# A two-layer trunk on one core: in the channel mixers, every other inner tile as seven block products, the residual kept in DRAM, and rho applied behind the second half

## The chip, the core and the metric

The kernel runs on one core of one Trainium2 chip. Such a core has a matrix engine (TensorE: PE in the profile, with PEld for its weight loads), three elementwise engines (VectorE: DVE; ScalarE: ACT; GpSimd: POOL), a queue that issues transfers (SyncE: SP), and DMA engines between DRAM and the on-chip memory SBUF. TensorE writes its results into PSUM, of which this program uses eight banks of 128 x 512 float32 in the channel mixers, and DVE and ACT read them there. Every engine works through its own instructions in order, and waits at semaphores for the others.

The metric is the device time of one execution in microseconds. Before the change it is 1362.86 us, the median of three runs (1361.54 to 1366.15).

## The reference

Two layers over 512 frames of width 1024. Layer 0 mixes time by a recurrence, layer 1 by chunked attention; the change touches neither. Each layer ends in a channel mixer with an inner width of 2816:

```python
def rms_norm(x, g):
    y = xf * lax.rsqrt(jnp.mean(xf * xf, axis=-1, keepdims=True) + RMS_EPS)
    return y * g

def conv_glu(h, w_in, conv_w, conv_b, w_out):
    gate, val = jnp.split(h @ w_in, 2, axis=-1)
    gp = jnp.pad(gate, ((0, 0), (CONV_W - 1, 0), (0, 0)))
    conv = conv_b + sum(conv_w[j] * gp[:, j:j + seq] for j in range(CONV_W))
    return (jax.nn.gelu(conv, approximate=False) * val) @ w_out

for layer in range(DEPTH):
    ...
    x = x + jnp.concatenate([mix, mo], axis=-1) @ w_out[layer]
    x = x + conv_glu(rms_norm(x, ln2[layer]), ffn_in[layer], ffn_conv[layer],
                     ffn_conv_b[layer], ffn_out[layer])
return rms_norm(x, ln_f)
```

## The kernel before, in words

Everything is stored with features on the 128 partitions and the 512 frames along the free axis: `xT`, the residual, is eight tiles of 128 x 512. A float32 product is made of three products of float32r halves: an operand is split into a rounded part (`whi`, `r1h`) and the rest (`wlo`, `r1l`), and `dense` (L189 to L204) issues, for every block of 128 input features, hi x hi (L198) and hi x lo (L199), and after all of them lo x hi (L203). One unit of eight blocks is thus 16 + 8 matmuls of 128 x 512.

A weight block is loaded by SP into `wraw` (L180, two buffers), cast by ACT to `whi` (L169) and subtracted by DVE to `wlo` (L175). `whi` and `wlo` have three buffers each, so the cast for a unit waits until the matmuls of the third unit before it have read theirs.

`ffn(l, ...)` is the channel mixer. Its input is x times the gain `ln2`, split, without the factor `rho` (the reciprocal root of the mean square, one number per frame), which commutes with the products and is multiplied in afterwards. It has two halves:

- The first half runs over 22 inner tiles j. Each makes two units, the gate into one PSUM bank (`psf`, four banks) and the value into another, then on DVE and ACT: gate times `rho` (L355), the three convolution taps (L357 ACT, L358 and L359 DVE), Gelu (L360 ACT), value times `rho` (L362), their product (L363), and its split into the hidden tile (L215 ACT, L216 DVE). Hidden tiles 0 to 7 lie in the pair of buffers that the other mixer stage uses (`r1h`/`r1l` or `r2h`/`r2l`), 8 to 21 in `f3h`/`f3l`.
- The second half runs over eight output tiles m, each 22 blocks (66 matmuls) into one of two banks `psd`, which DVE adds to `xT[m]` (L374); then the norm's squares and the next stage's input follow (`norm_tile`, L230 to L236).

In layer 1 the last output tile goes through `finish`: two halves of 256 frames, each 66 matmuls of 128 x 256, so that norm and output of the first half lie beside the matmuls of the second.

The Tile framework's scheduler decides the order on each engine from the order of the calls, the pools' buffers and its own estimates; the order is fixed when the program is built.

Of the kernel before, what the change touches and what calls it, by code (L numbers as in the profile page):

```python
# [39 lines left out]
for _n, _c in _VEC:  # L40
# [71 lines left out]
def trunk_kernel(ctx, tc, A, out):  # L112
# [13 lines left out]
    cst = cp.tile([P, NCST], F32, name="cst")  # L126
# [213 lines left out]
    def ffn(l, hp, act, h_, l_, xT, after, last=None):  # L340
        f3h = hp.tile([P, NFF - 8, S], F32R, name="f3h")
        f3l = hp.tile([P, NFF - 8, S], F32R, name="f3l")

# [3 lines left out]
        for j in range(NFF):  # L347
            wg = load_w(A["ffn_in"][l, j, 0])
            wv = load_w(A["ffn_in"][l, j, 1])
            pg = ps_f()  # L350
# [4 lines left out]
            V.tensor_tensor(g[:], pg[:], rho[:], op=ALU.mult)  # L355
# [4 lines left out]
            SC.activation(c[:], c[:], AF.Gelu)  # L360
# [2 lines left out]
            V.tensor_tensor(v[:], v[:], c[:], op=ALU.mult)  # L363
            split_to(*hid(j), v[:])
        for m in range(KD):
# [8 lines left out]
            V.tensor_tensor(xT[:, m], xT[:, m], ps[:], op=ALU.add)  # L374
            after(m)
# [928 lines left out]
```

## Time and profile before

| view | |
|---|---|
| median of 3 runs | 1362.86 us |
| the profiled execution | 1368.61 us, of which the span from first to last instruction 1366.8 |
| DVE | 827.0 us busy, 61% |
| ACT | 609.7 us busy, 45% |
| POOL | 35.2 us busy, 3% |
| DMA | 140.49 MB, mean 103 GB/s |
| 22 inner tiles of layer 0 | from 403.1 to 642.5 us |
| 8 output tiles of layer 0 | to 763 us |
| attention of layer 1 | to about 957 us |
| 22 inner tiles of layer 1 | from 963.7 to 1203 us |
| 8 output tiles of layer 1, norm and output | to the end |

The profile is one execution taken by the hardware profiler, and runs a little longer than the median run. Times in its rows are counted from the first instruction. In a row of the timeline stand start, duration, engine, line of the source, operation, what is written from what, shapes, how many such instructions the row holds, and in brackets how long the engine idled before it and what ended that. Engines start the next instruction before the last one has quite ended, so the distance from start to start is shorter than the duration: for one DVE instruction of 128 x 512 by some 0.08 us.

### The profile page before, as it was taken

How to read it: one execution, taken by the hardware profiler on the slowest of the kernel's cores; microseconds unless marked ns; L12 is line 12 of the kernel's file. 1: busy time of each engine (PE TensorE's matmuls, PEld its weight loads, DVE VectorE, ACT ScalarE, POOL GpSimd, SP SyncE). 2: the span in 40 equal slices, each digit the busy share in tenths (PEclk: the TensorE clock that was granted, in tenths of full speed). 3: DMA queues.
4: the chain of work that ended last, by engine and by line, in shares of the span. 5: the costliest groups of instructions: out<-in, count | busy, mean ns of one | idle time of the engine just before them, and what ended most of it. 6: DMA issues, size and time to landing. Idle time of an engine off the chain costs nothing.

```text
span 1366.8 us, 20878 instructions
## 1 busy us (share of the span) xinstructions
PE 1318.4 (96%) x8266; PEld 1072.8 (78%) x8266; DVE 827.0 (61%) x1751; ACT 609.7 (45%) x1019; POOL 35.2 (3%) x57
## 2 busy tenths in 40 slices
PE   6989999999999999999999999999999999999996
PEld 5777777776788888888888878786888888888886
DVE  7876888788565655655334666757665555653324
ACT  5556554545444333333222476657443333332221
POOL 3000000000000000000000000000000000000000
PEclk9999999999999999999999999999999999999998
DMA  5366544545222232223323422231322232232332
GB/s 182 105 187 138 106 100 96 126 109 131 78 93 93 93 107 94 93 98 97 85 85 111 133 86 87 92 115 63 108 93 93 93 108 93 93 94 87 108 85 75
DMA packets 64322, 140.49 MB, mean 103 GB/s; under 512 B 24672, under 2 KB 28896, under 8 KB 64224
## 3 DMA queue, kind: packets, MB, share of 16 engines
q1 hardware_dynamic: 61200, 128.15, 29.9%
q0 software_dynamic: 3024, 11.01, 4.7%
q8 instruction: 65, 1.06, 0.3%
q14 instruction: 33, 0.27, 0.1%
HBM read 132.32 MB, written 6.82 MB: 102 GB/s over the span
## 4 chain that ended last, share of the span: by engine, by line
PE 78%; DVE 12%; ACT 4%; DMA 3%; issue 2%; SPq 1%; DVEq 0%; ACTq 0%; POOLq 0%
PE psf L198 12%; PE psf L199 12%; PE psf L203 12%; PE psd L198 10%; PE psd L199 10%; PE psd L203 9%; DVE Xu L675 2%; DVE Xs L677 1%; PE pss L1121 1%; PE psl L203 1%; DMA d<-Xs 1%; PE pss L725 1%; DMA Tt<-d 1%; PE pss L297 1%; PE psd L1071 1%
## 5 line engine op out<-in xcount | busy, mean ns | idle before, releaser
L175 DVE TENSOR_TENSOR wlo<-wraw,whi 128x1024 fp32r<-128x1024 f32 (+1 forms) x181 | 216.5, 1196 | 134.0 <-PE psd L203 122.5
L169 ACT CAST whi<-wraw 128x1024 fp32r<-128x1024 f32 (+1 forms) x202 | 207.7, 1029 | 161.1 <-DMA wraw<-in_ffn_out_dram 40.0
L198 PE MATMUL psf<-r1h,whi 128*128 128x512 f32 x352 | 137.2, 390 | 0.0
L198 PE MATMUL psf<-r2h,whi 128*128 128x512 f32 x352 | 137.2, 390 | 0.0
L199 PE MATMUL psf<-r1l,whi 128*128 128x512 f32 x352 | 137.0, 389 | 0.0
L199 PE MATMUL psf<-r2l,whi 128*128 128x512 f32 x352 | 137.0, 389 | 0.0
L198 PE MATMUL psd<-r1h,whi 128*128 128x512 f32 x318 | 127.8, 402 | 1.2 <-ACT whi L169 1.2
L199 PE MATMUL psd<-r1l,whi 128*128 128x512 f32 x318 | 125.4, 394 | 0.0
L203 PE MATMUL psd<-r1h,wlo 128*128 128x512 f32 x318 | 86.7, 405 | 4.4 <-DMA wlo<-in_wA_dram 4.4
L199 PE MATMUL psd<-f3l,whi 128*128 128x512 f32 (+1 forms) x238 | 88.6, 377 | 0.0
L198 PE MATMUL psd<-f3h,whi 128*128 128x512 f32 (+1 forms) x238 | 88.6, 377 | 0.0
L362 DVE TENSOR_TENSOR tmp<-psf,rho 128x512 f32<-128x512 f32 x44 | 30.4, 691 | 94.6 <-PE psf L203 94.6
L203 PE MATMUL psf<-r1h,wlo 128*128 128x512 f32 x352 | 86.9, 389 | 0.0
L203 PE MATMUL psf<-r2h,wlo 128*128 128x512 f32 x352 | 86.9, 389 | 0.0
L198 PE MATMUL psd<-r2h,whi 128*128 128x512 f32 (+1 forms) x200 | 77.1, 389 | 0.8 <-ACT r2h L1128 0.7
L199 PE MATMUL psd<-r2l,whi 128*128 128x512 f32 (+1 forms) x200 | 76.4, 385 | 0.8 <-DVE r2l L216 0.8
L198 PEld LDWEIGHTS psf<-r1h,whi 128*128 128x128 f32 x352 | 66.1, 188 | 13.8
L203 PEld LDWEIGHTS psf<-r1h,wlo 128*128 128x128 f32 x352 | 66.1, 188 | 13.7
L203 PEld LDWEIGHTS psf<-r2h,wlo 128*128 128x128 f32 x352 | 66.1, 188 | 13.7
L198 PEld LDWEIGHTS psf<-r2h,whi 128*128 128x128 f32 x352 | 66.1, 188 | 13.7
L199 PEld LDWEIGHTS psf<-r2l,whi 128*128 128x128 f32 x352 | 66.1, 188 | 13.6
L199 PEld LDWEIGHTS psf<-r1l,whi 128*128 128x128 f32 x352 | 66.1, 188 | 13.6
(368 smaller groups left out, 2440.4 us busy)
## 6 DMA issues: line engine op xcount, KB each, us to landing
wraw<-in_ffn_in_dram SPq DMA_DIRECT2D x88, 512.0 KB, 3.2
wraw<-in_ffn_out_dram SPq DMA_DIRECT2D x32, 448.0 KB, 3.3
wraw<-in_wA_dram SPq DMA_DIRECT2D x20, 512.0 KB, 4.0
wlo<-in_wA_dram POOLq DMA_DIRECT2D x17, 512.0 KB, 8.2
wraw<-in_w_out_dram SPq DMA_DIRECT2D x16, 512.0 KB, 3.5
wraw<-in_ffn_out_dram SPq DMA_DIRECT2D x16, 512.0 KB, 4.3
wraw<-in_wB_dram SPq DMA_DIRECT2D x8, 512.0 KB, 3.4
Lr<-d SPq DMA_DIRECT2D x24, 128.0 KB, 5.4
```

The source lines that it names most:

```text
L169: SC.copy(hi[:, :n], raw)
L175: V.tensor_tensor(lo[:, :n], raw, hi[:, :n], op=ALU.subtract)
L198: PE.matmul(ps, wh[:, j * P:(j + 1) * P], ah, start=start and n == 0, stop=False)
L199: PE.matmul(ps, wh[:, j * P:(j + 1) * P], al, start=False, stop=False)
L203: PE.matmul(ps, wl[:, j * P:(j + 1) * P], act(k)[0], start=False, stop=stop and n == len(ks) - 1)
L297: PE.matmul(pso[hs, :], vm[l][:, kt, (f * 2 + hh) * 64:(f * 2 + hh + 1) * 64], pts[f, hh, kt], start=kt == 0, stop=kt == 1)
L362: V.tensor_tensor(v[:], pv[:], rho[:], op=ALU.mult)
L675: V.tensor_tensor(uv, L1.rearrange("p i o -> p o i").to_broadcast([P, k, n]), X[:, 0:k, q:q + 1].to_broadcast([P, k, n]), op=ALU.mult)
L677: V.tensor_tensor(X[:, 0:k, q + 1:], X[:, 0:k, q + 1:], uv, op=ALU.add)
L725: PE.matmul(ps[h][:, c], KB[HS[h], cc, 1 - h:3 - h].rearrange("p s t -> p (s t)"), AR[HS[h], cc].rearrange("p s t -> p (s t)"), start=True ...
L1071: PE.matmul(pt, r1h[:, k, ts], wh[:, ws], start=k == 0, stop=False)
L1121: PE.matmul(pso[HS[hh], kt * P:], vS[i // 2][:, kt, (i % 2 * 2 + hh) * 64:(i % 2 * 2 + hh + 1) * 64], pts[hh][:, kt, kt * P:], start=kt == ...
```

## The change

**Seven products.** For j = 4, 6, ..., 16 (seven tiles in each layer) the two units of an inner tile are computed as a 2 x 2 block product. The blocks of one factor are the input's upper and lower 512 features for the first and last 256 frames (B00, B10, B01, B11), those of the other the gate and value weights for the upper and lower features. Seven block products, each 4 blocks of 128 features in three passes, 12 matmuls of 128 x 256, replace eight. They need four sums of input blocks (T1 to T4) and sums of weight blocks: `seven` forms them from the raw weights on DVE and splits four sets, `wv`, `wg`, `wx` and `w4`. The products run as: b = B00·wv; c = T1·wg; b += T2·wx; a = B10·wv; b += T3·wx; b += T4·wg; c += B11·w4. After the first, second and third step ACT copies the running sum out of bank b (s0, s1, u0), DVE combines these copies with a and c, and matmuls go on adding into the same bank.

**Order.** `ffn` runs a seven up to T3, then the first 12 matmuls of the next tile's gate unit, then T4 and w4, then the rest of that tile.

**Sums of the input.** `sums`, called behind tiles 0 and 1, reads x back from DRAM, scales by `ln2`, forms T1 to T4 and splits them: the rounded parts into `xh`, which takes the place of `xT` in SBUF, the rests into slots of `f3h`/`f3l` that belong to hidden tiles 18 to 21.

**The residual.** POOL stores `xT` to DRAM (`xd`, 8 transfers) ahead of the mixer and loads it back behind tile 17 (8 transfers). To make room, the constants of which only the first layer has need (`cs2`) are in a tile of that stage.

**rho.** The value is no longer multiplied by `rho`; each of the second half's outputs is, ahead of the residual add (one DVE instruction more for each m, one less for each plain tile).

```diff
+    SEVEN = range(4, 18, 2)
+    HT = (slice(0, 256), slice(256, 512))
-    def ffn(l, hp, act, h_, l_, xT, after, last=None):
+    def ffn(l, hp, ih, il, h_, l_, xT, after, last=None):
...
+        xd = dp.tile([KD, P, S], F32, name="xd", tag="xd", bufs=2)
...
+        def sums(k):
+            u, w = tmp(), tmp()
+            for t_, q in ((u, k), (w, k + 4)):
+                nc.sync.dma_start(t_[:], xd[q])
+                SC.activation(t_[:], t_[:], AF.Copy, scale=Vc(f"ln2_{l}", q))
+            t12, t34 = tmp(), tmp()
+            V.tensor_tensor(t12[:, HT[0]], u[:, HT[1]], u[:, HT[0]], op=ALU.subtract)
...
+            for n, t_ in enumerate((t12, t34)):
+                split_to(high(k)[:, n], low(k)[:, n], t_[:])
...
+        def prod(ps, w, o, a, start=True):
+            wh, wl = w
+            for k in range(4):
+                ws = slice(o + k * P, o + k * P + P)
+                ah, al = a(k)
+                PE.matmul(ps, wh[:, ws], ah, start=start and k == 0, stop=False, skip_group_check=not start)
+                PE.matmul(ps, wh[:, ws], al, start=False, stop=False, skip_group_check=not start)
+            for k in range(4):
+                PE.matmul(ps, wl[:, o + k * P:o + k * P + P], a(k)[0], start=False, stop=k == 3,
+                          skip_group_check=not start)
...
+        def seven(j):
+            rv = hp.tile([P, 1024], F32, name="rv", tag="rv")
+            rg = hp.tile([P, 1024], F32, name="rg", tag="rg")
...
+            wv = split_w(rv[:], 1024)
+            V.tensor_tensor(rg[:, one], rg[:, one], rg[:, two], op=ALU.add)
+            wg = split2(own("wg", 1024), rg[:])
+            V.tensor_tensor(rg[:, one], rg[:, one], rv[:, one], op=ALU.subtract)
+            V.tensor_tensor(rg[:, two], rg[:, two], rg[:, one], op=ALU.subtract)
+            V.tensor_tensor(rv[:, two], rv[:, two], rg[:, one], op=ALU.subtract)
+            wx = split_w(rg[:], 1024)
+            w4 = split2(own("w4", 512), rv[:, two])
...
+            prod(b[:], wv, 0, B(0, 0))
+            SC.copy(s[:, HT[0]], b[:])
+            yield
+            prod(c[:], wg, 0, T(1))
+            prod(b[:], wx, 0, T(2), False)
+            SC.copy(s[:, HT[1]], b[:])
+            a = ps_f((P, 256))
+            prod(a[:], wv, 512, B(1, 0))
+            V.tensor_tensor(v[:, HT[0]], a[:], s[:, HT[0]], op=ALU.add)
+            prod(b[:], wx, 512, T(3), False)
+            u = tmp()
+            SC.copy(u[:, HT[0]], b[:])
+            V.tensor_tensor(u[:, HT[1]], c[:], u[:, HT[0]], op=ALU.add)
+            V.tensor_tensor(g[:, HT[1]], u[:, HT[1]], rho[:, HT[1]], op=ALU.mult)
+            yield
+            prod(b[:], wg, 512, T(4), False)
+            V.tensor_tensor(g[:, HT[0]], b[:], rho[:, HT[0]], op=ALU.mult)
+            prod(c[:], w4, 0, B(1, 1), False)
+            V.tensor_tensor(v[:, HT[1]], c[:], s[:, HT[1]], op=ALU.add)
+            gated(j, g, v[:])
...
+            if j == SEVEN[-1] + 1:
+                xT = mid.tile([P, KD, S], F32, name="xT", tag="xT")
+                for m in range(KD):
+                    GP.dma_start(xT[:, m], xd[m])
...
-            V.tensor_tensor(xT[:, m], xT[:, m], ps[:], op=ALU.add)
-            after(m)
+            t = tmp()
+            V.tensor_tensor(t[:], ps[:], rho[:], op=ALU.mult)
+            V.tensor_tensor(xT[:, m], xT[:, m], t[:], op=ALU.add)
+            after(xT, m)
```

What the scheduler makes of it is seen on the two engines that feed TensorE. On ACT before, one inner tile of layer 0 (hidden tile 13 from `tmp_5998`, tile 14's convolution in `tmp_6067`) has two casts of weights, the cast of the hidden tile, the first tap and Gelu:

```order
L169 CAST whi_6079<-wraw_6077 128x1024
L215 CAST f3h_4965<-tmp_5998 128x512
L169 CAST whi_6085<-wraw_6083 128x1024
L357 ACTIVATE tmp_6067<-tmp_6065,vec_67 128x512
L360 ACTIVATE tmp_6067<-tmp_6067 128x512
```

On ACT now, from the end of tile 7 through tile 8: `wraw_5842` and `wraw_5848` are the weights of tile 9, `rv_5950` and `rg_5951` those of tile 10, `psd_5769` is bank b of tile 8, `tmp_5736` and `tmp_5741` are tile 7's convolution and hidden tile, `tmp_5893` tile 8's convolution:

```order
L172 CAST whi_5844<-wraw_5842 128x1024
L388 ACTIVATE tmp_5736<-tmp_5736 128x512
L445 COPY tmp_5771<-psd_5769 128x256
L218 CAST r1h_68<-tmp_5741 128x512
L449 COPY tmp_5771<-psd_5769 128x256
L172 CAST whi_5850<-wraw_5848 128x1024
L172 CAST whi_5954<-rv_5950 128x1024
L455 COPY tmp_5838<-psd_5769 128x256
L218 CAST wgh_5959<-rg_5951 128x1024
L385 ACTIVATE tmp_5893<-tmp_5773,vec_67 128x512
L388 ACTIVATE tmp_5893<-tmp_5893 128x512
L172 CAST whi_5966<-rg_5951 128x1024
```

The copies of the running sum (L445, L449, L455) now stand between casts and Gelu, and matmuls that go on in the bank wait for each of them: the first stands behind tile 7's Gelu, the second behind the cast of tile 7's hidden tile, the third behind two casts of weights.

On DVE before, one inner tile (tile 5 of layer 0; `wlo_5420` and `wlo_5488` are rests of the weights of the tiles that follow):

```order
L355 TENSOR_TENSOR tmp_5399<-psf_5349,rho_71 128x512
L175 TENSOR_TENSOR wlo_5420<-wraw_5417,whi_5419 128x1024
L358 SCALAR_TENSOR_TENSOR tmp_5401<-tmp_5399,vec_67,tmp_5401 128x511
L359 SCALAR_TENSOR_TENSOR tmp_5401<-tmp_5399,vec_67,tmp_5401 128x510
L362 TENSOR_TENSOR tmp_5406<-psf_5374,rho_71 128x512
L175 TENSOR_TENSOR wlo_5488<-wraw_5485,whi_5487 128x1024
L363 TENSOR_TENSOR tmp_5406<-tmp_5406,tmp_5401 128x512
L216 TENSOR_TENSOR r1l_69<-tmp_5406,r1h_68 128x512
```

On DVE now, from tile 8's convolution (`tmp_5893`) to tile 9's (`tmp_5941`), with the weights of tile 10 between (`rg_5951`, `rv_5950`, `wlo_5967`, `w4l_5971`):

```order
L386 SCALAR_TENSOR_TENSOR tmp_5893<-tmp_5773,vec_67,tmp_5893 128x511
L435 TENSOR_TENSOR rg_5951<-rg_5951,rv_5950 128x512
L387 SCALAR_TENSOR_TENSOR tmp_5893<-tmp_5773,vec_67,tmp_5893 128x510
L436 TENSOR_TENSOR rg_5951<-rg_5951 128x512
L437 TENSOR_TENSOR rv_5950<-rv_5950,rg_5951 128x512
L390 TENSOR_TENSOR tmp_5898<-tmp_5772,tmp_5893 128x512
L405 TENSOR_TENSOR tmp_5939<-psf_5854,rho_71 128x512
L178 TENSOR_TENSOR wlo_5967<-rg_5951,whi_5966 128x1024
L219 TENSOR_TENSOR f3l_4968<-tmp_5898,f3h_4967 128x512
L386 SCALAR_TENSOR_TENSOR tmp_5941<-tmp_5939,vec_67,tmp_5941 128x511
L219 TENSOR_TENSOR w4l_5971<-rv_5950,w4h_5970 128x512
L387 SCALAR_TENSOR_TENSOR tmp_5941<-tmp_5939,vec_67,tmp_5941 128x510
```

The sums of weights and two of the four splits have moved between the taps of tiles 8 and 9; tile 9's second tap (the last row) now has eleven instructions ahead of it that were not there or stood elsewhere, and tile 9's Gelu on ACT waits for it.

More of the change, by code (lines that the diff above doesn't have):

```diff
@@ L125, in trunk_kernel @@
     open_banks(ctx, D=2)
[L126 removed]
+    cst = cp.tile([P, NCST0], F32, name="cst")
+    cs2 = []
     vec = cp.tile([P, NVEC], F32, name="vec")
@@ L360, in ffn, with eight @@
             SC.activation(c[:], c[:], AF.Gelu)
-            v = tmp()
-            V.tensor_tensor(v[:], pv[:], rho[:], op=ALU.mult)
-            V.tensor_tensor(v[:], v[:], c[:], op=ALU.mult)
-            split_to(*hid(j), v[:])
+            o = tmp()
+            V.tensor_tensor(o[:], v, c[:], op=ALU.mult)
+            split_to(*hid(j), o[:])
+        def eight(j):
+            wg = load_w(A["ffn_in"][l, j, 0])
+            wv = load_w(A["ffn_in"][l, j, 1])
+            pg = ps_f()
+            n = 0
+            for _ in dense(pg[:], [(wg, K8)], act):
+                n += 1
+                if n == 2:
+                    yield
+            pv = ps_f()
+            run(dense(pv[:], [(wv, K8)], act))
+            g = tmp()
+            V.tensor_tensor(g[:], pg[:], rho[:], op=ALU.mult)
+            gated(j, g, pv[:])
@@ new lines, in ffn @@
+        for m in range(KD):
+            GP.dma_start(xd[m], xT[:, m])
+        xh.append(mid.tile([P, KD, S], F32R, name="xh", tag="xT"))
+        rest = None
+        for j in range(NFF):
+            t = (seven if j in SEVEN else eight)(j)
+            next(t)
+            if rest is not None:
+                run(rest)
+                rest = None
+            if j in SEVEN:
+                next(t)
+                rest = t
+            else:
+                run(t)
+            if j < 2:
+                sums(2 * j)
+                sums(2 * j + 1)
+            if j == SEVEN[-1] + 1:
+                xT = mid.tile([P, KD, S], F32, name="xT", tag="xT")
+                for m in range(KD):
+                    GP.dma_start(xT[:, m], xd[m])
@@ L1201, in store @@
                 x_ = xT[:, m, ht]
-                V.tensor_tensor(x_, x_, pss[u][:], op=ALU.add)
+                t = tmp()
+                V.tensor_tensor(t[:, :256], pss[u][:], rho[:, ht], op=ALU.mult)
+                V.tensor_tensor(x_, x_, t[:, :256], op=ALU.add)
                 sq = tmp()
@@ L1220, in finish @@
             run(store(1))
-        ffn(1, hp, act1, r2h, r2l, xT, after, finish)
+        ffn(1, hp, r1h, r1l, r2h, r2l, xT, after, finish)
 def _wtile(w, nf=P):
```

71 lines of the change are left out of this document (47 added, 24 removed).

## The prediction

> **What bounds the kernel now.** I read the page's busy times first, then the waits of TensorE, then busy times over chosen stretches.
>
> ```profile
> span 1366.8 us, 20878 instructions
> PE 1318.4 (96%) x8266; PEld 1072.8 (78%) x8266; DVE 827.0 (61%) x1751; ACT 609.7 (45%) x1019; POOL 35.2 (3%) x57
> PE pss L255 <- DVE tmp L252: 2.9, 2, 2.6
> 403.10:642.50 239.40, 239.40 (x1063) 198.17 (x1062) 141.94 (x188) 90.88 (x113) 0.00 (x0) 1.00 0.29 95
> 500.00:510.88 10.88, 10.88 (x49) 9.01 (x48) 6.35 (x9) 4.06 (x5) 0.00 (x0) 1.00 0.29 99
> ```
>
> The third row is TensorE's longest wait from 395 us to the end: 2.9 us in total, two times. The fourth is the inner loop of layer 0 (stretch, its length, then busy us of PE, PEld, DVE, ACT, POOL, then granted clock): TensorE is busy for all 239.40 us at clock 1.00, while DVE has 141.94 and ACT 90.88. So the mixers run at the pace of matmuls. A matmul saved is time saved, until DVE or ACT cannot keep up. The fifth row is one tile: 10.88 us, DVE 6.35, ACT 4.06.
>
> Busy time of pipelined matmuls doesn't price one; the distance between starts does. The last output tiles happen to hold both shapes:
>
> ```profile
> 1321.58 0.39 PE L198 MATMUL psd<-r2h,whi 128*128 128x512 f32 x1
> 1333.36 3.34 PE L203 MATMUL psd<-f3h,wlo 128*128 128x512 f32 x14
> 1336.54 0.28 PE L198 MATMUL psd<-r2h,whi 128*128 128x256 f32 x1
> 1341.81 1.12 PE L203 MATMUL psd<-r2h,wlo 128*128 128x256 f32 x8
> 1344.45 0.28 PE L198 MATMUL psd<-r2h,whi 128*128 128x256 f32 x1
> 1346.57 0.36 PE L198 MATMUL psd<-r2h,whi 128*128 128x256 f32 x1
> 1346.77 0.28 PE L199 MATMUL psd<-r2l,whi 128*128 128x256 f32 x1
> 1336.50:1344.40 7.90, 7.90 (x67) 7.86 (x66) 2.47 (x3) 2.20 (x3) 0.00 (x0) 1.00 0.12 49
> ```
>
> One output tile of 66 matmuls of 128x512 lasts from 1321.58 to 1336.54: 14.96 / 66 = 0.2267 us each. The next 66, of 128x256, last to 1344.45: 7.91 / 66 = 0.1198. Half the columns cost 53%, at the same clock 1.00 (last row).
>
> **The change part by part.**
>
> *Matmuls.* A plain tile has 48 of 128x512: 48 x 0.2267 = 10.88 us, as the row of one tile says. A seven has 7 x 12 = 84 of 128x256: 84 x 0.1198 = 10.07. That is 0.81 us, or 7.5% of a tile where the count of products promises 12.5%, because the narrow matmul carries its fixed part more often. Fourteen such tiles: **-11.4 us**. This is the whole gain; all else can only take from it.
>
> Each product also ends one run of matmuls and starts another with a wait. From the wide to the narrow shape no gap shows: 1333.36 + 14 x 0.2267 = 1336.53. After the tiny norm matmuls the first narrow one lasts 1346.77 - 1346.57 = 0.20, that is 0.08 more. For 14 x 7 product starts the bounds are 0 and 98 x 0.08 = 7.8 us; I take 0, the row nearest in kind, since all products are float32r streams.
>
> [...]
>
> *DVE and ACT per pair of tiles.* Prices, from one tile before and from the end of the kernel:
>
> ```profile
> 508.14 0.69 DVE L355 TENSOR_TENSOR tmp<-psf,rho 128x512 f32<-128x512 f32 x1 [1.64 <-PE psf L203]
> 508.75 1.22 DVE L175 TENSOR_TENSOR wlo<-wraw,whi 128x1024 fp32r<-128x1024 f32 x1
> 509.88 0.75 DVE L358 SCALAR_TENSOR_TENSOR tmp<-tmp,vec 128x511 f32<-128x511 f32 x1
> 510.66 0.75 DVE L359 SCALAR_TENSOR_TENSOR tmp<-tmp,vec 128x510 f32<-128x510 f32 x1
> 505.16 0.62 ACT L215 CAST f3h<-tmp 128x512 fp32r<-128x512 f32 x1 [2.69 <-DVE tmp L363]
> 506.32 1.05 ACT L169 CAST whi<-wraw 128x1024 fp32r<-128x1024 f32 x1 [0.55 <-PE psf L199]
> 508.87 0.82 ACT L357 ACTIVATE tmp<-tmp,vec 128x512 f32<-128x512 f32 x1 [1.49 <-DVE tmp L355]
> 511.50 0.63 ACT L360 ACTIVATE tmp<-tmp 128x512 f32<-128x512 f32 x1 [1.82 <-DVE tmp L359]
> 1349.79 0.37 ACT L256 COPY rho<-pss 128x256 f32<-128x256 f32 x1 [3.72 <-PE pss L255]
> 1352.10 1.84 PE L203 MATMUL psd<-f3h,wlo 128*128 128x256 f32 x14
> 1353.97 0.42 DVE L1202 TENSOR_TENSOR xT<-xT,psd 128x256 f32<-128x256 f32 x1 [1.42 <-PE psd L203]
> ```
>
> From start to start DVE needs 0.61 for 128x512 (508.14 to 508.75), 1.13 for 128x1024, 0.67 for a tap (0.78 if it needs the one before), and 0.34 for 128x256 (0.42 less the 0.08). A seven has three splits of 1024 (3.4), four sums of 512 and the split of w4 (3.0), five pieces of 256 (1.7), two taps, a product and a hidden split (2.6): 10.7 us. The plain tile beside it loses L362: 6.35 - 0.69 = 5.7. A pair is 16.4 us of DVE in 10.07 + 10.88 = 20.95 of TensorE; ACT has some 10. Sums alone hide. What decides is whether the copies out of the running bank are in time.
>
> I walk the steady pair of the order's rows, with 0 at the end of T4 of a seven j. TensorE then runs: w4 to 1.44; the rest of the gate unit of j+1 (12 matmuls, 2.72) to 4.16; its value unit (24, 5.44) to 9.60; the next seven's first product to 11.04; T1 to 12.48; T2 to 13.92; a to 15.36; T3 to 16.80; 12 wide ones to 19.52; T4 to 20.96. A reader starts 0.19 after the last matmul's slot (1352.10 + 14 x 0.1198 = 1353.78, and DVE at 1353.97). DVE: gate half at 0.2, the split of wg at 0.8 (its cast on ACT ends at 0.77), the value half at 1.95, then the twelve quoted rows, with hardly a gap, from 2.3; the last, tile j+1's second tap, ends at 10.6. Gelu on ACT to 11.2, **first copy** to 11.65; T2 wants it at 12.48: slack 0.8. **Second copy**: T2's end + 0.2 = 14.1 to 14.5, the cast ahead of it done at 13.0; T3 wants it at 15.36: slack 0.8. **Third copy**: behind the cast of tile j+4's value weights (its buffer is free when T3's hi pass is read, 16.5) to 17.6, copy to 17.95; T4 wants it at 19.52: slack 1.6. Every wait is covered, the narrowest by 0.8 us in 21. If cover goes, every us beyond it is a us of idle TensorE, fourteen times.
>
> The first two sevens of a layer have another order and two long casts closer to the copies. Walked from 403.08 in the same way, only two waits of about 0.1 us come out: **+0.3** for both layers.
>
> *Sums of the input.* Eight calls, each 4 x 0.34 + 2 x 0.61 = 2.6 us of DVE, four of them in tiles 0 to 3 of each layer, where DVE has 10.88 - 5.7 = 5.2 free per tile: 0. Their loads stand on SP behind weight loads already prefetched. The casts to `xh` wait for all eight stores of the residual, and hold ACT if these are late:
>
> ```profile
> 403.28 0.69 DVE L337 TENSOR_TENSOR xT<-xT,psd 128x512 f32<-128x512 f32 x1 [2.35 <-PE psd L203]
> wlo<-in_wA_dram POOLq DMA_DIRECT2D x17, 512.0 KB, 8.2
> wraw<-in_ffn_in_dram SPq DMA_DIRECT2D x88, 512.0 KB, 3.2
> ```
>
> The last tile of x is done at 403.97, and the walk has the first cast at 423. A POOL transfer took 8.2 us with twice the bytes and an accumulate; issued as the tiles become ready, the stores are done by some 413. The seven's raw weights have one buffer, so the next load is issued when the last split is done (8.0 in the walk); with 3.2 us to land it is there at 11.6, and its first sum stands on DVE at 12.3.
>
> *Second half.* One DVE instruction more per m, 0.61 in 14.96 us: hidden by the matmuls of the next m, except at the ends. At the very end the 256-wide one stands between the last matmul and the add (row 1353.97): **+0.45**. At the end of layer 0:
>
> ```profile
> 764.46 0.68 DVE L374 TENSOR_TENSOR xT<-xT,psd 128x512 f32<-128x512 f32 x1
> 767.02 1.02 PE L245 MATMUL pss<-cst,acc 128*128 128x2 f32 x8
> ```
>
> the add now stands behind the new multiplication and a weight split that the scheduler put between: 0.61 + 1.13 = 1.74 us later, and with it the norm's matmuls at 767.02, rho and the first attention scores. TensorE gets six matmuls of the K projection (1.4 us) ahead of the norm. Bounds 0 and 1.7; I take the middle, **+0.8**.
>
> *Elsewhere.* The recurrence keeps its order but for a few rows, attention shifts by some; the same work: 0, give or take 1.5.
>
> **Sum:** -11.4 + 0.3 + 0.45 + 0.8 = **-9.9 us**. The profiled span would be 1366.8 - 9.9 = 1356.9, the profiled execution 1368.61 - 9.9 = 1358.7; that execution lies 5.75 above the median of the runs, so the median comes to 1362.86 - 9.9 = **1353.0 us**, 0.7% less. A measurement of this kernel tells about 0.3% from no change, 4.1 us: below 1358.8 is faster, above 1367 slower.
>
> **Rivals.**
>
> *DVE sets the pair's pace.* The loop from T4 by way of DVE, Gelu and first copy to the next T4 is 11.65 + 8.48 (T2, a, T3, 12 wide, T4) = 20.1 us against TensorE's 20.96. For it: DVE is filled from 2.0 to 10.6. Against: all durations are measured ones. It decides once the loop is 0.8 longer (8 us of DVE work being a tenth slower); 1.6 longer and the pair gains nothing. Half to all of the gain lost, with the costs above: 1358 to 1364. Chance 0.13.
>
> *The stores are late: slower.* If each of the eight takes the full 8.2 us and they follow one another from 380 on, the last lands at 446, ACT stands at the first cast from 423, and the casts for tile 3's weights, due by 436, come 13 us late, in both layers: 1353 + 26 = 1379. It decides from 5.3 us a store. Nothing in this profile shows a plain store on that queue; half the bytes speak against. With smaller delays 1365 to 1380, chance 0.06.
>
> *Weight loads show.* If a load could not lie beside the matmul ahead of it, a narrow matmul would take at least the load's time:
>
> ```profile
> L203 PEld LDWEIGHTS psd<-f3h,wlo 128*128 128x128 f32 x56 | 8.8, 190 | 1.1
> ```
>
> 84 x 0.190 = 15.96 against 10.88, +5.1 a tile: 1363 + 71 = 1434. Against it: the lo pass at 1341.81, where every matmul has other weights, takes 1344.45 - 1341.81 = 2.64 for 22, 0.12 each, with loads of 190 ns beside. Chance 0.02. [...]
>
> *Product starts cost* near their upper bound of 7.8 us: 1357 to 1361, chance 0.05. That fewer matmuls are not issued is excluded: the order has 84 for each seven.
>
> **How the numbers follow.** The forecast as it stands (1349.5 to 1357.5) has 0.74; the rivals 0.13, 0.06, 0.02 and 0.05. Up to 1363, the range leaves out a little above and below: about 0.1. Faster: 0.74 and a few hundredths of the first and last rival, 0.78; slower 0.08; the same 0.14.
>
> **What would show it.** TensorE's page row should have 8266 + 14 x 36 = 8770 matmuls, DVE some 90 us more, ACT 60 more. Between tiles 8 and 17 a pair should last 20.95 us with PE busy throughout, and the waits should hold no PE entry at L413 or L414 above 1 us in total. Wrong would be: idle PE at L413 ahead of T2 or T3, released by ACT L445 or L449 (DVE's pace); a long ACT wait at the first cast to `xh` released by a DMA (stores); starts farther apart than 0.12 inside a product (loads); or a longer attention stage.

## The result, and the profile after

The changed kernel takes 1353.12 us (median of 6 runs, 1349.61 to 1356.96), the kernel before 1364.20 in the 6 runs beside it (1361.54 to 1367.90). The ratio is 0.9916, 95% interval 0.9893 to 0.9940: faster by 0.6 to 1.1%. The prediction was 1353.0.

The top of the page of the changed kernel, engines with busy time, share of the span and instructions:

```profile
span 1350.4 us, 22292 instructions
PE 1305.3 (97%) x8770; PEld 1085.4 (80%) x8770; DVE 901.2 (67%) x1912; ACT 663.2 (49%) x1121; POOL 53.0 (4%) x89
```

The 8770 matmuls are there; DVE has 74 us more (some 90 were expected), ACT 53 (60).

The profiled spans differ by 16.4 us, more than the runs do. To see where, I cut each profile at three first matmuls: the gates of layer 0 (`psf<-r2h`), the hidden tiles of layer 0's second half (`psd<-f3h`; eight blocks lie ahead of it in that half, which in the kernel before begins at 643.9 us, not at the 642.5 of the table ahead of the prediction), and the gates of layer 1 (`psf<-r1h`); the fourth cut is the last hi x hi matmul on `psd<-f3h`. The instructions of one source line hold all four cuts: per group its count, durations in ns, then first and last start. Changed kernel, then the kernel before:

```profile
L201 PE MATMUL psf<-r2h,whi x240: 389/389/486, 396.0 to 629.5; 128*128 128x512 f32 x120
L201 PE MATMUL psf<-r1h,whi x240: 387/389/481, 979.3 to 1212.8; 128*128 128x512 f32 x120
L201 PE MATMUL psd<-f3h,whi x238: 279/389/389, 635.4 to 1334.1; 128*128 128x512 f32 x105, 128*128 128x256 f32 x14
```

```profile
L198 PE MATMUL psf<-r2h,whi x352: 388/389/478, 403.1 to 641.7; 128*128 128x512 f32 x176
L198 PE MATMUL psf<-r1h,whi x352: 387/389/486, 990.9 to 1229.5; 128*128 128x512 f32 x176
L198 PE MATMUL psd<-f3h,whi x238: 279/389/390, 647.6 to 1350.9; 128*128 128x512 f32 x105, 128*128 128x256 f32 x14
```

In the same way every run of this study was cut (us; the last column is the span less the first):

| kernel | up to the first gate | gates, layer 0 | to the gates of layer 1 | second mixer | tail | behind the first gate |
|---|---|---|---|---|---|---|
| before | 403.1 | 244.5 | 343.3 | 360.0 | 15.9 | 963.7 |
| before_again | 401.7 | 244.5 | 343.4 | 360.0 | 15.9 | 963.8 |
| **changed** | 396.0 | 239.4 | 343.9 | 354.8 | 16.3 | 954.4 |
| no_sevens | 397.4 | 244.5 | 343.9 | 359.9 | 16.4 | 964.7 |
| eight_narrow | 400.3 | 249.1 | 343.8 | 364.4 | 16.8 | 974.1 |
| copy2 | 394.0 | 240.2 | 343.7 | 355.6 | 16.3 | 955.8 |
| copy6 | 397.4 | 241.8 | 343.6 | 357.3 | 16.3 | 959.0 |
| gate_again3 | 400.0 | 248.3 | 343.8 | 362.1 | 16.3 | 970.5 |
| ten_sevens | 396.2 | 248.3 | 343.4 | 365.2 | 16.6 | 973.5 |
| fourteen_sevens | 396.4 | 266.0 | 343.7 | 380.1 | 16.4 | 1006.2 |
| rho_value | 394.7 | 241.2 | 342.9 | 356.7 | 15.8 | 956.6 |
| eight_sevens | 402.1 | 238.6 | 345.6 | 354.1 | 16.4 | 954.7 |
| eight_rho_value | 395.7 | 240.6 | 342.8 | 356.0 | 15.9 | 955.3 |

What lies behind the first gate repeats to a tenth of a us between the two profiles of the kernel before; the stage ahead of it varies by 9 us over programs that differ little there. So the stages are the instrument here: the changed kernel is 9.3 us shorter behind the first gate (-5.1, +0.6, -5.2, +0.4), and the other 7.1 us of the two profiles are the first stage.

One steady pair of tiles in the changed kernel, TensorE's first matmul of some products and ACT's part (timeline; the columns are those of the prediction's rows). On TensorE these are the first product, T2, T3, the first of the twelve wide matmuls behind T3, T4, and the first product of the next pair:

```profile
504.26 0.28 PE L413 MATMUL psd<-r2h,whi 128*128 128x256 f32 x1
...
507.13 0.28 PE L413 MATMUL psd<-xh,whi 128*128 128x256 f32 x1
...
510.01 0.28 PE L413 MATMUL psd<-xh,whi 128*128 128x256 f32 x1
...
511.45 0.40 PE L201 MATMUL psf<-r2h,whi 128*128 128x512 f32 x1
...
514.20 0.28 PE L413 MATMUL psd<-xh,wgh 128*128 128x256 f32 x1
...
525.25 0.28 PE L413 MATMUL psd<-r2h,whi 128*128 128x256 f32 x1
```

```profile
505.89 0.37 ACT L445 COPY tmp<-psd 128x256 f32<-128x256 f32 x1 [0.18 <-PE psd L416]
...
508.77 0.37 ACT L449 COPY tmp<-psd 128x256 f32<-128x256 f32 x1 [1.40 <-PE psd L416]
...
512.12 0.37 ACT L455 COPY tmp<-psd 128x256 f32<-128x256 f32 x1
```

The pair lasts 525.25 - 504.26 = 20.99 us. The copies end at 506.26, 509.14 and 512.49, and T2, T3 and T4 begin at 507.13, 510.01 and 514.20: slack 0.87, 0.87 and 1.71 (the walk had 0.8, 0.8 and 1.6). TensorE was busy throughout (the stretch from one T4 to the next; columns as in the prediction):

```profile
493.20:514.20 21.00, 21.00 (x134) 19.08 (x133) 16.64 (x25) 10.65 (x15) 0.00 (x0) 1.00 0.31 98
```

### The profile page after: what moved, and what is told of

It reads as the page before. It is cut to its first block, busy times and chain, and to the rows that moved or that the text cites. A ratio compares the mean times of both kernels' runs of the same rounds, so it can differ in the third digit from the quotient of the medians.

```text
span 1350.4 us, 22292 instructions
## 1 busy us (share of the span) xinstructions
PE 1305.3 (97%) x8770; PEld 1085.4 (80%) x8770; DVE 901.2 (67%) x1912; ACT 663.2 (49%) x1121; POOL 53.0 (4%) x89
## 4 chain that ended last, share of the span: by engine, by line
PE 80%; DVE 12%; ACT 4%; issue 2%; DMA 2%; SPq 0%; DVEq 0%; ACTq 0%; POOLq 0%
PE psd L201 10%; PE psd L202 10%; PE psd L206 10%; PE psf L201 8%; PE psf L202 8%; PE psf L206 8%; PE psd L413 2%; PE psd L416 2%; PE psd L414 2%; DVE Xu L802 2%; PE psf L416 1%; PE psf L414 1%; PE psf L413 1%; DVE Xs L804 1%; PE pss L1248 1%
## 5 line engine op out<-in xcount | busy, mean ns | idle before, releaser
L172 ACT CAST whi<-wraw 128x1024 fp32r<-128x1024 f32 (+1 forms) x174 | 179.0, 1030 | 278.4 <-DMA wraw<-in_ffn_out_dram 112.7
L178 DVE TENSOR_TENSOR wlo<-wraw,whi 128x1024 fp32r<-128x1024 f32 (+1 forms) x153 | 182.4, 1192 | 142.8 <-PE psd L206 83.8
L201 PE MATMUL psf<-r2h,whi 128*128 128x512 f32 x240 | 93.7, 390 | 0.0
L201 PE MATMUL psf<-r1h,whi 128*128 128x512 f32 x240 | 93.7, 390 | 0.0
L202 PE MATMUL psf<-r2l,whi 128*128 128x512 f32 x240 | 93.6, 390 | 0.0
L202 PE MATMUL psf<-r1l,whi 128*128 128x512 f32 x240 | 93.6, 390 | 0.0
L206 PEld LDWEIGHTS psd<-r1h,wlo 128*128 128x128 f32 x318 | 58.2, 191 | 16.7 <-DMA wlo<-in_wA_dram 4.5
L201 PEld LDWEIGHTS psd<-r1h,whi 128*128 128x128 f32 x318 | 59.7, 188 | 14.5 <-ACT whi L172 1.3
L202 PEld LDWEIGHTS psd<-r1l,whi 128*128 128x128 f32 x318 | 59.8, 188 | 11.5 <-issue 0.2
L206 PE MATMUL psd<-f3h,wlo 128*128 128x512 f32 (+1 forms) x238 | 53.7, 377 | 0.0
```

The source lines that it names most:

```text
L172: SC.copy(hi[:, :n], raw)
L178: V.tensor_tensor(lo[:, :n], raw, hi[:, :n], op=ALU.subtract)
L201: PE.matmul(ps, wh[:, j * P:(j + 1) * P], ah, start=start and n == 0, stop=False)
L202: PE.matmul(ps, wh[:, j * P:(j + 1) * P], al, start=False, stop=False)
L206: PE.matmul(ps, wl[:, j * P:(j + 1) * P], act(k)[0], start=False, stop=stop and n == len(ks) - 1)
```

## The experiments

In the diffs, + and - are against the changed kernel. Ratios are to the kernel before, with 95% intervals.

### no_sevens: everything but the sevens

```diff
-    SEVEN = range(4, 18, 2)
+    SEVEN = ()
...
-            if j == SEVEN[-1] + 1:
+            if j == 17:
```

> The changed kernel with no seven at all: every inner tile has its 48 wide matmuls, while the sums of the input, the residual's way through DRAM, the order of the calls and rho behind the second half stay (the sums are then read by nothing). My account: all of the gain is matmuls not issued, and the rest only costs: the tail 0.45 us, the end of layer 0 about 0.6 to 0.8, 0 elsewhere. So against the kernel before +1 to +1.5 us (ratio 1.001), and by stages from the first matmul of a mixer to the first of its second half on f3h 244.5 us as before, not the 239.4 of the changed kernel. Rival, the stages outside the mixers brought part of the gain (the stage ahead of the first mixer was 7 us shorter in the changed kernel's profile, 396.0 against 403.1): 5 to 7 us faster than before, ratio 0.995, with a first mixer that starts at 396.

1365.58 us (median of 12), ratio 1.0011 (0.9991 to 1.0031). The gate stage is 244.5 again, the two costs are there (343.9, 16.4), and behind the first gate it is 1.0 us longer than before. So the gain is in the sevens alone, and the store, the sums and the reloads cost nothing that the stages show. A first stage that was truly 5 us shorter would have given -4 us, ratio 0.997, outside the interval: the 397.4 is a draw of that stage, as is the 403.1.

### before_again: the first stage

The kernel before once more, one run with a profile.

> The kernel before once more, for a second profile of it. The stage ahead of the first mixer ended at 403.1 us in the first profile, and at 394.0 to 400.3 in five profiles of the changed kernel and its variants, whose programs are the same there but for some rows. If that is only the spread of executions, this one too lies within some 394 to 403, not nearer to 403 than the others do; if the change shortened that stage, near 403 again. The stages behind it should repeat to some tenths: 244.5, 343.3 and 360.0 us.

401.7, 244.5, 343.4, 360.0. Behind the first gate all repeats. The first stage came nearer to 403 than I had named for mere spread (403.1 and 401.7 here, 394.0 to 402.1 in eleven others), so its profiles alone don't exclude an effect of some us. The time of no_sevens, in which that stage is as in the changed kernel, excludes one of 5 us; its interval leaves room for some 2.

### eight_narrow: the price of the shape and of a product's start

```diff
+            if j in NARROW:
+                for c in range(2):
+                    prod(pg[:, HT[c]], wg, 0, B(0, c))
...
+                    prod(pg[:, HT[c]], wg, 512, B(1, c), False)
+                for c in range(2):
+                    prod(pv[:, HT[c]], wv, 0, B(0, c))
+                    prod(pv[:, HT[c]], wv, 512, B(1, c), False)
```

> As no_sevens, but tiles 4, 6, ..., 16 of each layer make their two units as eight block products of 12 matmuls of 128x256, 96 in place of 48 wide ones; no sums are used, the result is the same. My account: a narrow matmul costs 0.1198 us wherever it stands and a product's start costs nothing, so such a tile lasts 96 x 0.1198 = 11.50 us against 10.88, +0.62, and the kernel 14 x 0.62 = +8.7 us against no_sevens, about +10 against before (ratio 1.007). Rival, half the columns are half the price and the seven's saving was 12.5% less something else: the same time as no_sevens. Rival, every product start costs 0.08 us: 112 starts, 9 us more than my figure, about +19 against before (ratio 1.014).

1376.1 us, ratio 1.0084 (1.0052 to 1.0116); 9.4 us more than no_sevens behind the first gate. The start of a narrow tile, of the plain one behind it, and of the next narrow one (timeline of TensorE):

```profile
445.27 0.28 PE L424 MATMUL psf<-r2h,whi 128*128 128x256 f32 x1
456.79 0.40 PE L201 MATMUL psf<-r2h,whi 128*128 128x512 f32 x1
467.69 0.28 PE L424 MATMUL psf<-r2h,whi 128*128 128x256 f32 x1
```

96 narrow matmuls in eight products last 11.52 us, 0.1200 each; 48 wide ones 10.90. Eight starts cost at most 11.52 - 11.50 = 0.02 us together. Both rivals (half price; 0.08 a start) fall. The shape alone makes a tile 5.7% longer, and seven of the eight products last 7/8 x 11.52 = 10.08 us, 7.5% less than the wide tile.

### copy2 and copy6: how much cover the second copy has

```diff
-            SC.copy(s[:, HT[1]], b[:])
+            for _ in range(3):
+                SC.copy(s[:, HT[1]], b[:])
```

(copy6: 7 in place of 3.)

> The changed kernel with ACT's second copy out of the running bank done three times in place of once (same source, same target). By the walk the second copy ends 0.8 us before T3 wants the bank; two more of some 0.28 us from start to start use 0.56 of it. My account: no change against the changed kernel (1353 us, ratio 0.992 to before), steady pairs of 21.0 us. Rival, the copies are already on the path and every us on ACT counts: 14 x 0.56 = +7.8 us (ratio 0.998), pairs of 21.6.

1355.26 us, ratio 0.9927 (0.9903 to 0.9952). Gate stage 240.2 against 239.4: 0.1 us a pair. The copies cost more than I had estimated, and used the cover up to the last tenth (copy2, timeline):

```profile
507.17 1.18 ACT L450 COPY tmp<-psd 128x256 f32<-128x256 f32 x3 [1.40 <-PE psd L416]
...
508.41 0.38 PE L413 MATMUL psd<-xh,whi 128*128 128x256 f32 x1
508.63 0.28 PE L414 MATMUL psd<-f3h,whi 128*128 128x256 f32 x1
```

Three copies into one target take 1.18, that is (1.18 - 0.37) / 2 = 0.405 apart, not 0.28. They end at 508.35 and T3 begins at 508.41: 0.81 us spent of the 0.87. T3's second matmul starts 0.22 behind its first in place of 0.12, and this is the 0.1 by which the pair is longer. The slack of the walk is real.

> The changed kernel with the second copy done seven times; the order on ACT then also puts one weight cast (0.95 us from start to start) among the copies. My account: the last copy ends 6 x 0.28 + 0.95 = 2.6 us later than now, 0.8 of it covered, so TensorE waits 1.8 us ahead of T3 in every seven, 14 x 1.8 = +25 us against the changed kernel: about 1378 (ratio 1.011), pairs of 22.8 us and a wait of some 25 us in total at the matmuls behind the copies. Rival, TensorE's waiting is made up elsewhere in the pair, since ACT and DVE have free time there: under +5 us. Rival, no cover at all: 14 x 2.6 = +37 us (1390).

1357.93 us, ratio 0.9957 (0.9934 to 0.9980): gate stage 241.8, second mixer +2.5, so 4.9 us in the two mixers and not 25. The rival that named under 5 had the size right. The extra 6 x 0.405 and a cast in between are all there, but TensorE hardly stands (copy6, one pair, then rows of its timeline):

```profile
506.52:527.90 21.38, 21.33 (x133) 18.92 (x132) 15.77 (x24) 11.66 (x21) 0.00 (x0) 1.00 0.29 99
```

```profile
517.42 1.18 ACT L450 COPY tmp<-psd 128x256 f32<-128x256 f32 x3
518.22 0.39 PE L201 MATMUL psf<-r2h,whi 128*128 128x512 f32 x1
518.65 0.39 PE L413 MATMUL psd<-xh,whi 128*128 128x256 f32 x1
518.88 0.28 PE L414 MATMUL psd<-f3h,whi 128*128 128x256 f32 x1
```

The order of TensorE's work, which the program's scheduler makes from its own estimates, had changed: of the plain tile's wide matmuls, eleven stand ahead of T2 and sixteen between T2 and T3, under the copies; three are left between T3 and T4, where the changed kernel has twelve. This is the order of the program, not something TensorE does while it runs, and not free time of ACT and DVE as the rival had it. Of the 0.38 by which the pair is longer, 0.31 stand at T3, for which the last copies are just too late: it starts 0.43 behind the wide matmul ahead of it in place of 0.23, and its second matmul 0.23 behind its first in place of 0.12.

### gate_again3: more work on DVE

```diff
             V.tensor_tensor(g[:], pg[:], rho[:], op=ALU.mult)
+            for _ in range(3 if 4 < j < 17 else 0):
+                V.tensor_tensor(g[:], pg[:], rho[:], op=ALU.mult)
             gated(j, g, pv[:])
```

(It acts in tiles 5, 7, ..., 15; tile 17 is not among them, unlike what the expectation says.)

> The changed kernel with DVE's first gate instruction of the plain tiles 5, 7, ..., 17 (gate times rho) done four times in place of once: 3 x 0.61 = 1.83 us more of DVE in a pair, 18.2 in 21.0, all ahead of that tile's taps and Gelu. Two accounts of cover. By the walk of the prediction, with every instruction at its place: the extra 1.83 us and the weight splits that the scheduler now puts among them make Gelu and the first copy behind it some 4.7 us later, 1.0 us of it covered, so TensorE waits 3.7 us ahead of T2 in 12 pairs: +44 us against the changed kernel (about 1397). By what copy6 showed, that the scheduler moves wide matmuls ahead of the product that would have to wait: what counts is that DVE has 18.2 us of work in a pair of 21.0, and the loss stays under 8 us (1353 to 1361, ratio up to 0.998).

1369.21 us, ratio 1.0047 (1.0028 to 1.0066): 16.1 us more behind the first gate, between the two accounts. A steady pair lasts 22.07 us, and DVE has 18.43 in it, so it is not DVE's rate; nor are the copies late. The wait is another one, made by the new order (gate_again3, the stretch of one pair, then its timeline):

```profile
534.87:556.94 22.07, 21.35 (x134) 18.90 (x132) 18.43 (x28) 10.37 (x16) 0.00 (x0) 1.00 0.31 97
```

```profile
538.90 1.05 ACT L172 CAST whi<-wraw 128x1024 fp32r<-128x1024 f32 x1 [2.98 <-PE psf L416]
...
540.07 0.47 PE L201 MATMUL psf<-r2h,whi 128*128 128x512 f32 x1 [0.72 <-ACT whi L172]
```

The wide matmuls of the plain tile had been moved up to cover the late copy, and now wait 0.72 us for their own weights: the cast to `whi` needs a buffer that the product just before them sets free (2.98 us of waiting for TensorE). In the third pair of each layer a gate bank that DVE held for the repeated instructions stopped TensorE for 2.31 us (section on the hardware).

### ten_sevens and fourteen_sevens: is DVE the limit?

```diff
-    SEVEN = range(4, 18, 2)
+    SEVEN = (4, 5, 7, 8, 10, 11, 13, 14, 16, 17)
```

(fourteen_sevens: `range(4, 18)`; both run the last seven to its end behind tile 17.)

> Ten sevens in each layer in place of seven: tiles 4, 5, 7, 8, 10, 11, 13, 14, 16, 17, two of three. If TensorE stays the bound: 6 more x 0.81 = -4.9 us against the changed kernel (1348, ratio 0.988), three tiles lasting 2 x 10.07 + 10.88 = 31.0 us while DVE has 2 x 10.7 + 5.7 = 27.1. I expect some of it lost, since the second of two sevens finds single buffers: its set wg can be cast only when T4 of the first is through, 0.95 us of ACT with 1.44 us of TensorE (w4) ahead of T1, then the rest of it on DVE; up to 0.5 us for each of 10 neighbours, so -5 to 0. Rival, the copies and DVE's pace decide already (DVE 10.7 in the second seven of 10.07): 0.6 to 2 us lost at each neighbour, 6 to 20 us slower than those -4.9, that is 1354 to 1368.

1371.82 us, ratio 1.0059 (1.0041 to 1.0077): slower than no seven at all, and above both of the ranges that I had named. The group of three tiles lasts 33.07 us, not 31.0 (ten_sevens, one group):

```profile
509.50:542.57 33.07, 32.07 (x217) 29.38 (x216) 27.52 (x42) 16.88 (x25) 0.00 (x0) 1.00 0.28 98
```

DVE has 27.52 of it, so it is not its rate either. Of the 2.07 us too much, about 1.1 stand at the start of T2 of the second seven (ten_sevens, timeline of ACT, DVE and TensorE):

```profile
519.57 1.05 ACT L218 CAST wgh<-rg 128x1024 fp32r<-128x1024 f32 x1 [0.53 <-PE psd L414]
520.65 1.23 DVE L219 TENSOR_TENSOR wgl<-rg,wgh 128x1024 fp32r<-128x1024 f32 x1 [0.17 <-ACT wgh L218]
...
524.11 1.05 ACT L172 CAST whi<-rg 128x1024 fp32r<-128x1024 f32 x1 [2.72 <-DVE rg L436]
...
525.20 0.39 PE L413 MATMUL psd<-xh,whi 128*128 128x256 f32 x1 [0.88 <-ACT whi L172]
```

The set `wg` has one buffer, free when T4 of the first seven has been read; only then come its cast (519.57) and its split (520.65), then the sums in the same raw tile (L436), then the cast for `wx` (524.11), and T2 waits for it. Behind T2's start another 0.6 us goes at its lo x hi pass and at the next wide weights, whose split and cast stand behind this chain; some 0.3 stand at T3 of the first seven. I had named the start of the chain and priced it at up to 0.5 us; it goes on through the raw tile, and costs about 1.7.

> Every tile from 4 to 17 a seven, 14 in each layer. TensorE would have 10.07 us a tile: 14 x 0.81 = -11.4 against the changed kernel (1342), if nothing else held it. DVE has 10.7 us of work in each, so at best 10.7 a tile, 0.2 more than now on average (10.48): +6 us, 1359. With the single buffers of the weight sets and no wide matmuls to put ahead of a waiting product I expect 11 to 12 a tile: +15 to +43 us, 1368 to 1396, DVE over 90% busy in that stretch or waiting for ACT and TensorE in turn. So: near 1342 the bound is TensorE; 1359 DVE's rate alone; above it the chain of waits.

1404.71 us, ratio 1.0303 (1.0282 to 1.0323), above DVE's rate as expected, but also above the 11 to 12 us a tile and the 1396 us that I had named: 12.37 us a tile with 11.03 of DVE (fourteen_sevens, the stretch of a tile, then TensorE's waits in its timeline):

```profile
529.61:541.98 12.37, 11.15 (x87) 10.33 (x85) 11.03 (x18) 6.43 (x10) 0.00 (x0) 1.00 0.23 86
```

```profile
534.04 0.39 PE L413 MATMUL psd<-xh,whi 128*128 128x256 f32 x1 [0.25 <-ACT whi L172]
...
536.49 0.38 PE L413 MATMUL psd<-xh,whi 128*128 128x256 f32 x1 [0.46 <-ACT tmp L449]
...
538.64 0.39 PE L413 MATMUL psd<-xh,wgh 128*128 128x256 f32 x1 [0.46 <-ACT tmp L455]
```

Here T2, T3 and T4 follow one another with a bare copy between, since the product a, which stands ahead of T3 in the changed kernel, has moved ahead of T2, whose weights come late. From T3's start to T4's is 538.64 - 536.49 = 2.15 us where 12 matmuls take 1.44: a bare copy out of the running bank costs 0.7 us. Two of them are 1.4 us, more than the 0.81 that a seven saves; most of the rest of the 2.30 above 10.07 stands at T2's weights. In the changed kernel, where the sevens pay, other matmuls stand ahead of T2, T3 and T4 (slack 0.87, 0.87 and 1.71): its own T1 and a for the first two, the plain tile's for T4.

### rho_value: undo the move of rho

```diff
-            gated(j, g, pv[:])
+            v = tmp()
+            V.tensor_tensor(v[:], pv[:], rho[:], op=ALU.mult)
+            gated(j, g, v[:])
...
             V.tensor_tensor(v[:, HT[1]], c[:], s[:, HT[1]], op=ALU.add)
+            V.tensor_tensor(v[:], v[:], rho[:], op=ALU.mult)
...
-            t = tmp()
-            V.tensor_tensor(t[:], ps[:], rho[:], op=ALU.mult)
-            V.tensor_tensor(xT[:, m], xT[:, m], t[:], op=ALU.add)
+            V.tensor_tensor(xT[:, m], xT[:, m], ps[:], op=ALU.add)
...
```

(The last lines left out do the same for the two halves in `finish`.)

> The changed kernel with its seven sevens, but rho where it was before: on the value of every inner tile, ahead of the product with the gate (0.69 us of DVE for a plain tile, 0.61 for a seven, 1.3 in a pair), and no multiplication in the second half. It tests the two terms that the prediction charged to the move. My account: the end of layer 0 gets the 0.6 us back (343.3 in place of 343.9 from the first f3h matmul of layer 0 to the first psf matmul of layer 1) and the tail 0.4 (15.9 in place of 16.3), while DVE's 17.7 us in a pair of 21.0 stay covered, some tenths lost: 1352.5, the mixers' first half 239.4 to 240.5. Rival, DVE's pace: every us on it is paid, 14 x 1.3 = 18 us less the cover of 0.8 to 1.0 in each of 12 to 14 pairs: first half up to 3 us longer in each layer, 1357 to 1359.

1354.8 us, ratio 0.9944 (0.9931 to 0.9958). The two costs of the move are confirmed: without it the end of layer 0 is 1.0 shorter (342.9) and the tail 0.5 (15.8). But the gates take 1.8 and 1.9 us longer, more than I allowed and less than the rival's 3. The steady pair hardly changes; most of it is one wait for ACT as the sevens begin, in tile 5 (rho_value, the stretch of a steady pair, then a row of the timeline):

```profile
504.41:525.49 21.08, 21.08 (x133) 18.92 (x132) 17.98 (x28) 10.80 (x16) 0.00 (x0) 1.00 0.31 101
```

```profile
445.40 0.47 PE L201 MATMUL psf<-r2h,whi 128*128 128x512 f32 x1 [1.19 <-ACT r1h L218]
```

So the move pays 2.2 us net (956.6 against 954.4).

### eight_sevens and eight_rho_value

```diff
-    SEVEN = range(4, 18, 2)
+    SEVEN = range(4, 20, 2)
```

(eight_rho_value has this edit and that of rho_value.)

> One seven more in each layer, tile 18, with a plain tile between as everywhere: 4, 6, ..., 18; the residual comes back behind tile 19. My account: what counts is a plain tile between two sevens, so the eighth pays as the others do: 2 x 0.81 = -1.6 us against the changed kernel, the first half 238.6 in place of 239.4 us, about 1351.5 (ratio 0.991). Rival, the later return of the residual (8 transfers from DRAM two tiles later) is late for the first add of the second half, or tile 18's place among the slots of T's rests makes a wait: 0 to +5 us, seen as a longer stage behind the first half.

1355.99 us, ratio 0.9948 (0.9930 to 0.9966). The eighth seven pays as forecast: 238.6 and 354.1, -0.8 and -0.7. But the stage behind is 1.7 longer, so that 954.7 stands against 954.4. It is neither the residual's return nor a slot: at the end of layer 0 the norm's second matmuls wait 2.14 us for DVE (0.38 in the changed kernel). DVE's order there is the same in both. In it a split of attention's weights stands ahead of the norm's last steps, and here that split waits for a cast which waits for the weights' transfer (eight_sevens, then the cast in the changed kernel):

```profile
767.64 1.05 ACT L172 CAST whi<-wraw 128x1024 fp32r<-128x1024 f32 x1 [2.70 <-DMA wraw<-in_w_kvv_dram]
768.72 1.22 DVE L178 TENSOR_TENSOR wlo<-wraw,whi 128x1024 fp32r<-128x1024 f32 x1 [1.86 <-ACT whi L172]
...
770.69 0.63 PE L258 MATMUL pss<-cst,tmp 128*128 128x128 f32 x4 [2.14 <-DVE tmp L255]
```

```profile
759.96 1.05 ACT L172 CAST whi<-wraw 128x1024 fp32r<-128x1024 f32 x1 [0.22 <-DMA wraw<-in_w_kvv_dram]
```

One of the transfers of `in_w_kvv` took 6.3 us to land in this profile, none over 4.4 in the changed kernel's. With one profile of eight_sevens it stays open whether the eighth seven has to do with that.

> Both at once: eight sevens in each layer and rho on the value. If the parts add up: -1.6 and -1.0 us against the changed kernel, 1350.5 (ratio 0.990), stages 238.6, 343.3, a second mixer 0.8 shorter than the changed kernel's 354.8, and 15.9. Rival, DVE's pace as in rho_value, in one pair more.

1353.5 us, ratio 0.9935 (0.9921 to 0.9949); 955.3 behind the first gate. Its end of layer 0 is 342.8, without that wait, but the gates pay rho_value's price (240.6). No version here beats the changed kernel by anything that the runs can tell.

## Why the prediction was right, step by step

| step | predicted, us | measured, us |
|---|---|---|
| 14 sevens by 84 narrow for 48 wide, and 0.3 for the first two of a layer | -11.1 | -10.3 (-5.1 and -5.2) |
| product starts | 0 of at most 7.8 | 0 (0.02 for eight starts) |
| store, sums, reload | 0 | 0 (no_sevens: 244.5, 359.9) |
| end of layer 0 | +0.8 of at most 1.7 | +0.6 |
| tail | +0.45 | +0.4 |
| sum | -9.9 | -9.3 behind the first gate; -11.1 between the medians |

The mechanism held, and so did the size of the terms, but for 0.8 us in the first. That 1353.0 lies 0.1 us from the measured median is luck: the runs of the changed kernel spread over 7 us, and the kernel before came out 1.3 us above the 1362.86 from which the sum started.

**Matmuls.** Right: 0.1198 and 0.2267, read from the last two tiles of the kernel before, hold for the sevens, and eight_narrow shows them by themselves. From these two prices an estimated 2 x 0.1198 - 0.2267 = 0.013 us of a matmul does not shrink with its columns. The term is 0.8 us too large. Six pairs from the first seven on last 126.23 us, not 6 x 20.95 = 125.70: the first two last 21.10 and 21.14, each of the others 21.00. Of the 0.05 in a steady pair, 0.03 lies in the twelve wide matmuls behind T3, which take 514.20 - 511.45 = 2.75 and not 12 x 0.2267 = 2.72; the change from the narrow shape to the wide one, which the prediction put at nothing, is not quite free.

```profile
441.02 0.28 PE L413 MATMUL psd<-r2h,whi 128*128 128x256 f32 x1
567.25 0.28 PE L413 MATMUL psd<-r2h,whi 128*128 128x256 f32 x1
```

**Cover.** The walk gave the copies' slack to 0.1 us, and copy2 shows that it is all there is. What it could not give is what happens once the slack is exceeded: with the order as written each us would count, but a changed program is given a new order. Twice (copy6, gate_again3) the wide matmuls went to where the cover was missing. In copy6 only 0.3 us a pair was left to pay; in gate_again3 the price came from somewhere else, a weight buffer. The rival "DVE sets the pace" did not come true, and in none of the runs was DVE's rate the limit: where DVE held TensorE up, it was by a single wait.

**Rho.** The two costs were right. The step's flaw is that the move was charged with them alone: that it takes 1.3 us of DVE out of each pair was used in the walk, but what the walk would be with it was not worked out. rho_value shows 3.7 us.

**Stores.** Read from the changed kernel, the transfers to `xd` (first and last issue, then their landing), and the first cast of the sums in the timeline:

```profile
L466 POOL DMA_DIRECT2D xd<-xT x16: 539/542/583, 373.8 to 980.4; - x16
DMA to landing us min/median/max: 2.3/2.5/7.3
```

```profile
416.17 1.14 ACT L218 CAST xh<-tmp 128x512 fp32r<-128x512 f32 x2 [1.68 <-DVE tmp L378]
```

The median of 2.5 us is under the 5.3 from which the rival decided (the longest store, 7.3, is over it), and the cast waits for DVE, not for a transfer.

**Weight loads.** No load showed. In T2 of the steady pair each matmul has its own load, and loads and matmuls alike start 0.12 apart, though a load lasts 0.19 (changed kernel, timeline of the weight loads, then of TensorE):

```profile
507.01 0.19 PEld L413 LDWEIGHTS psd<-xh,whi 128*128 128x128 f32 x1
507.13 0.19 PEld L414 LDWEIGHTS psd<-f3h,whi 128*128 128x128 f32 x1
507.25 0.19 PEld L413 LDWEIGHTS psd<-xh,whi 128*128 128x128 f32 x1
```

```profile
507.13 0.28 PE L413 MATMUL psd<-xh,whi 128*128 128x256 f32 x1
507.25 0.28 PE L414 MATMUL psd<-f3h,whi 128*128 128x256 f32 x1
507.37 0.28 PE L413 MATMUL psd<-xh,whi 128*128 128x256 f32 x1
```

Had the loads been paid singly, the 84 of a seven would have lasted 84 x 0.19 = 16 us. From T2 to T3, two products, are 510.01 - 507.13 = 2.88 us, which makes 10.08 for seven.

**The base.** The profiled execution of before lay 5.75 us above the median, and the prediction kept that distance for the changed kernel: span 1356.9. It came to 1350.4, since the stage ahead of the first gate took 396.0 us this time and not 403.1; the forecast of the median does not rest on it. By the stages the gain is 9.3, by the medians 11.1, with an interval of 8.2 to 14.6 us.

## What to carry to other kernels

Price a narrower matmul by the distance of starts in a stretch of the same kernel that has both shapes: 12.5% fewer multiplications were worth 7.5% of the tile, and without the products saved the shape alone loses 5.7%. An accumulation that is read half way needed independent matmuls to run during every read (without them 0.7 us each in fourteen_sevens), and single buffers made a chain between neighbours (about 1.7 us of each group of three tiles in ten_sevens), so a scheme that paid on every other tile lost on every tile: 12.37 us a tile against the plain one's 10.88. Compare stages between profiles, not spans, when one stage varies by more than the change is worth; and when an experiment adds work, look first whether the order has changed with it.

## What the runs showed of the hardware that was not expected

In gate_again3 TensorE stood for about 2.3 us, and a us after it had started again its matmuls of 128x512 came 0.43 us apart in place of 0.23, for 3.4 us (timeline, then that stretch with its eight such starts and its granted clock of 0.50):

```profile
494.35 0.47 PE L201 MATMUL psf<-r2h,whi 128*128 128x512 f32 x1 [2.31 <-DVE tmp L407]
...
495.35 0.62 PE L201 MATMUL psf<-r2h,whi 128*128 128x512 f32 x1
```

```profile
495.35:498.75 3.40, 3.40 (x9) 2.66 (x8) 2.64 (x5) 0.89 (x2) 0.00 (x0) 0.50 0.77 260
```

Behind this wait of 2.3 us about 1.6 us more were lost (8 matmuls x 0.2), while the repeated waits of 0.7 in the same kernel left the clock at 1.00 (the steady pair from 534.87 to 556.94). But behind the same wait in layer 1 no matmul was slow (gate_again3: that wait; then the wide hi x hi matmuls of the gates in layer 0 and in layer 1 with their shortest, median and longest duration in ns, and these two waits in sum):

```profile
1086.50 0.47 PE L201 MATMUL psf<-r1h,whi 128*128 128x512 f32 x1 [2.31 <-DVE tmp L407]
```

```profile
L201 PE MATMUL psf<-r2h,whi x240: 387/389/632, 400.0 to 642.4; 128*128 128x512 f32 x120
L201 PE MATMUL psf<-r1h,whi x240: 387/389/486, 992.1 to 1232.9; 128*128 128x512 f32 x120
...
  DVE tmp L407: 4.6, 2
```

The slow matmuls of layer 0 are the ones that last up to 632 ns; in layer 1 none of this group lasts over 486. The stages agree: against the changed kernel the gates of layer 0 are 8.9 us longer and the second mixer 7.3, that is 1.6 less. So the length of the wait alone does not decide; what does, these two waits do not show.

The second surprise is in copy2: ACT's copies of 128x256 from PSUM into one target are 0.405 us apart, more than one takes alone (0.37), where I had estimated 0.28 (near the 0.37 less the 0.10 by which the copy at 512.12 starts ahead of the end of the cast at 511.17, which lasts 1.05; changed kernel); in copy6 four of them take 1.59 us, again 0.41 apart.
